# Two hybrid decoder layers: a gate tile asked for between the state-space halves, the first weights between the halves of x, decay and rate products of stacked exact parts, lag products in four runs

## The chip, the cores and the metric

The kernel runs on one core of a Trainium2 chip. The metric is the device time of one execution in microseconds (us); the time of a kernel is the median of its runs. Five engines work side by side, each through its own list of instructions in order: PE (TensorE, matrix products), DVE (VectorE), ACT (ScalarE), POOL (GpSimd) and SP (SyncE, which here starts the transfers).

## The reference

x (512 tokens by 1024 channels, float32) goes through two layers. Each layer projects x once and runs three token mixers on the projection; gates merge them, and a projection, two layer norms and an MLP follow. Shapes: A has 8 heads of 64; B 4 heads of 128 and 256; C 32 groups of 16 channels with 64 complex states each.

```python
proj = x @ w_in[l]
z_a, q_b, k_b, v_b, g_b, u_c, gate_logits = split(proj)
# A, rwkv7: zw, za, zg are 64, 64 and 128 columns of the token-shifted z_a
w_ll = -softplus(-(w0 + tanh(zw) @ w2)) - 0.5      # decay, w2 is 64 x 512
a = sigmoid(a0 + za @ a2)                          # rate,  a2 is 64 x 512
...                                                # delta rule over time
# B: retention.  C, state space: x[t] = ab * x[t-1] + bb @ u[t] (complex, diagonal)
y = gelu(real(c @ x) + d_skip * u)
y_c = y * sigmoid(y @ w_glu + b_glu)
merged = gate_a * (y_a @ wb_a) + gate_b * (y_b @ wb_b) + gate_c * (y_c @ wb_c)
x = layer_norm(alpha * x + merged @ w_out[l])
x = layer_norm(alpha * x + square(relu(x @ w_ff1[l])) @ w_ff2[l])
```

## The kernel before

**Large products.** Activations are held as a high part and a rest (xh, xl), both in a shortened float32 that TensorE multiplies exactly; weights too (wh, wl). A product is then three matmuls: wh by xh (L169), wh by xl (L170), wl by xh (L171). Weights come in blocks of 0.5 MB: `wblk` starts the transfer into raw (L148), ACT casts raw to wh (L151), DVE subtracts to wl (L155). raw, wh and wl each have three buffers in turn. A block of 128 channels gives 24 matmuls of 512 columns into one bank of the accumulator memory.

**Order.** A scheduler takes the recorded instructions, follows dependencies and priorities, and writes each engine's list; `ahead` raises the priority of what is recorded inside it, and `after` adds a dependency between two instructions. In the middle of a layer `weave` sets PE's order by hand: the chains of A and B are generators that yield (PE time, wait), and a filler of large matmuls (gates, B's projection, branch products) is put between their pieces.

**Start.** Four tiles of x (xin) are loaded, transposed on PE (`put_xT`, L219, four matmuls per accumulator bank, two banks per tile), cast and split. The three first weight blocks of u (the state space's columns) are loaded behind them on SP's list. For u each block is worked through in two halves of 256 tokens.

**State space (C).** `s5_prep` makes matrices from the parameters while PE runs u's and A's projections: transposes L402 (eight groups of four per layer) and, into one bank, the lag products L411 (32 matmuls of 32 rows by 128 per layer; a run of four is one value of (m, part)). `s5_main` works on two halves of the states: products with u (L460) into banks m and p, scans and twists on DVE that end in x (tiles cx, last instruction L484), then y of the half in two banks b: 64 matmuls of 64 columns on cx (L490) and 32 on u (L495); then gelu (L500 to L504) writes cy. Banks b are two, so y of half 1 can be written when gelu of half 0 has read both. The first three gate tiles (`gates`, L1088; each 24 large matmuls, then a tanh on ACT) are recorded behind `s5_main`, and the scheduler fills PE's waits with them. `s5_glu` follows.

**Decay and rate (A).** `a_proj` leaves the 128 rows of tanh(zw) and za in one float32 tile. `a_prep` of each of the four pairs of heads multiplies them with w2a2 (w2 and a2 stacked, loaded in `a_setup`, L633 and L634): one float32 matmul of the upper 64 rows (L671), one of the lower 64 (L675), 512 columns each, each into a bank m (of two). The bank is read by ACT. Ahead of them stand products of the pair before (L776, AVX, also into a bank m, read by ACT L777).

Of the kernel before, what the change touches and what calls it, by code (L numbers as in the profile page):

```python
# [11 lines left out]
F32 = mybir.dt.float32  # L12
# [68 lines left out]
class Hybrid:  # L81
# [61 lines left out]
    def wblk(self, src, a_, b_, extra=None):  # L143

        nc = self.nc
        with self.ahead(-2000000):
# [159 lines left out]
    def s5_prep(self, pool, keep):  # L306
# [64 lines left out]
        for d, b in zip(bd, (bre, bim)):  # L371
            G.memset(d, 0.0)
            for h in range(2):
                S.copy(out=d[H[h], :, h, :], in_=b[H[h]])

# [3 lines left out]
        for q in range(4):  # L379
# [16 lines left out]
            mix(self.ca[1][:, r], 9, 0, cim, cre, ADD, neg=True)  # L396
            for part, (x_, y_, op) in enumerate(((bre, bim, SUB), (bim, bre, ADD))):
                bp = t("bp", (128, 4, 8, 16))
                mix(bp, 8, 0, x_, y_, op)
                ps = self.mps()  # L400
                for i in range(4):
                    PE.transpose(ps[:, 128 * i:128 * i + 128], bp[:, i].rearrange("p b c -> p (b c)"), self.ident)  # L402
                S.copy(out=self.ba[:, part, r, :], in_=ps.rearrange("p (i s) -> p i s", i=4))

        gs = t("gs", (128, 4, 256))
        G.memset(gs[:, :, 0:128], 0.0)
        ps = self.pps().rearrange("p (m x) -> p m x", m=4)
        for m in range(4):
            for part in range(2):
                for j in range(4):  # L410
                    PE.matmul(ps[32 * j:32 * j + 32, m, :], lhsT=bd[part][:, 4 * m + j].rearrange("p g c -> p (g c)"),  # L411
                              rhs=self.ca[part][:, 4 * m + j, 0:8, :].rearrange("p k c -> p (k c)"), start=part == 0,
                              stop=part == 1, tile_position=(0, 32 * j))
        S.copy(out=gs[:, :, 128:256], in_=ps)
# [10 lines left out]
    def s5_u(self, pool):  # L425
# [9 lines left out]
        blocks = [self.wblk(w[:, :, C_U + 128 * i:C_U + 128 * i + 128], 8, 128) for i in range(3)]  # L435
# [9 lines left out]
    def s5_main(self, pool, keep):  # L445
# [7 lines left out]
        for hf in range(2):  # L453
# [31 lines left out]
            yp = [self.bps(), self.bps()]  # L485
# [6 lines left out]
            for g in range(2):  # L492
                for i in range(8):
                    gr = 2 * (8 * hf + i) + g
                    PE.matmul(yp[g][:, 64 * i:64 * i + 64], lhsT=self.tt[:, gr, :], rhs=self.uc[:, gr, :],  # L495
                              start=False, stop=True, skip_group_check=True)
            for g in range(2):

                ps, y, g1 = yp[g], page("cy", 2), page("cg1")
                S.activation(g1, ps, AF.Square)  # L500
                V.tensor_scalar(g1, g1, 0.044715, 1.0, op0=MUL, op1=ADD)
# [101 lines left out]
    def a_proj(self, pool, gp):  # L603
# [6 lines left out]
        def consume(i, ps):  # L610
            az, bg = dict(tag="az%d" % max(0, i - 11), bufs=1), dict(tag="bg", bufs=3)
            t, s = (p.tile([128, T], F32, name=self.nm(n), **k) for p, n, k in
                    ((gp, "az", bg) if i < 12 else (pool, "az", az), (pool, "azs", az) if i < 12 else (gp, "azs", bg)))
# [6 lines left out]
            elif i == 12:  # L620
                nc.scalar.activation(t[0:64], t[0:64], AF.Tanh)
                self.zwa = t
# [7 lines left out]
    def a_setup(self, pool):  # L630
        nc, par = self.nc, self.par
        self.w2a2 = pool.tile([128, T], F32, tag="w2a2", name=self.nm("w2a2"))
        nc.sync.dma_start(out=self.w2a2[0:64], in_=self.a["a_w2"][self.l])  # L633
        nc.sync.dma_start(out=self.w2a2[64:128], in_=self.a["a_a2"][self.l])  # L634
# [9 lines left out]
        for s in self.sbd:  # L644
            nc.gpsimd.memset(s, 0.0)

    def a_prep(self, pool, keep, p):
# [23 lines left out]
        PE.matmul(ps, lhsT=self.w2a2[0:64, 128 * p:128 * p + 128], rhs=self.zwa[0:64, :], start=True, stop=True)  # L671
# [3 lines left out]
        PE.matmul(ps, lhsT=self.w2a2[64:128, 128 * p:128 * p + 128], rhs=self.zwa[64:128, :], start=True, stop=True)  # L675
# [10 lines left out]
        yield 1.7, 1.0  # L686
# [93 lines left out]
    def a_inv(self, pool, p):  # L780
# [6 lines left out]
        NL = page("NL", 2, (128, 16, 16))  # L787
# [14 lines left out]
    def a_post(self, pool, p, bank):  # L802
# [71 lines left out]
        GM = page("GM", 2, (128, 8, 128))  # L874
# [283 lines left out]
    def layer(self, l):  # L1158
# [4 lines left out]
        if l == 0:  # L1163
            with tc.tile_pool(name="xin", bufs=1) as xin:
                self.new_xT()
                for t in range(4):
                    x = xin.tile([128, D], F32, tag="xin", bufs=4, name=self.nm("xin"))
                    with self.ahead(-3000000):
                        nc.sync.dma_start(out=x, in_=src[128 * t:128 * t + 128])
                    self.put_xT(t, x)  # L1170
# [178 lines left out]
```

## Time and profile before

| | us |
|---|---|
| median of 3 runs | 2098.81 |
| the runs | 2094.45, 2098.81, 2101.46 |
| the profiled execution, its own time | 2095.62 |
| its span in the profile | 2093.8 |

| engine | busy share of the span |
|---|---|
| PE | 98% |
| DVE | 58% |
| ACT | 35% |
| POOL | 7% |

A row of a timeline is: start, duration, engine, line, operation, tile written, tiles read, tile sizes, number of instructions in the group, and in brackets how long the engine was idle before it and what ended that. Matmuls overlap, so a group's duration is longer than the distance to the next one; distances between starts are used below. One operation of float32 can show as more than one matmul record. PEclk is TensorE's granted clock as a share of 2.4 GHz, 0.50 is 1.2 GHz.

### The profile page before, as it was taken

What the parts mean: (1) busy time and instruction counts of PE and PEld (TensorE: products, weight loads), DVE (VectorE), ACT (ScalarE), POOL (GpSimd) and SP (SyncE); (2) the same over time, 40 slices, a digit from 0 to 9 for tenths busy, and PEclk for the clock granted to TensorE, in tenths of its full rate; (3) what the DMA queues carried; (4) which work ended last, traced back from release to release, by engine and by line L of the source; (5) the groups of instructions that cost most, each with busy time, mean ns of one, the idle gap of its engine ahead of it and who ended that gap; (6) DMA issues with size and microseconds to landing.
All of it is one profiled execution on the core that took longest, in us unless ns stands there. A gap on an engine that the chain in (4) does not pass through costs nothing.

```text
span 2093.8 us, 31704 instructions
## 1 busy us (share of the span) xinstructions
PE 2061.0 (98%) x12784; PEld 1705.9 (81%) x12784; DVE 1217.3 (58%) x2048; ACT 741.4 (35%) x1079; POOL 147.8 (7%) x302
## 2 busy tenths in 40 slices
PE   8999999999999999999999999999999999999998
PEld 7788888788877888888887888888888878888886
DVE  7763567785566634344596644687856666343345
ACT  5433443434232423233244234344443324132231
POOL 0300022022000000000013000221120000000000
PEclk9998999999999999999999999999999999999999
DMA  9694643423645323233275856433336534223231
GB/s 221 155 140 142 183 127 82 112 78 88 223 150 177 113 79 121 81 100 110 93 159 158 127 151 183 123 94 88 100 113 191 178 130 140 79 93 101 91 121 50
DMA packets 365170, 263.95 MB, mean 126 GB/s; under 512 B 79328, under 2 KB 309856, under 8 KB 364896
## 3 DMA queue, kind: packets, MB, share of 16 engines
q1 hardware_dynamic: 365024, 261.93, 45.0%
q8 instruction: 100, 1.64, 0.3%
q14 instruction: 46, 0.38, 0.1%
HBM read 218.89 MB, written 42.99 MB: 125 GB/s over the span
## 4 chain that ended last, share of the span: by engine, by line
PE 86%; DVE 6%; DMA 3%; ACT 2%; issue 2%; SPq 1%; DVEq 0%; ACTq 0%
PE g L169 24%; PE g L170 24%; PE g L171 24%; PE b L1048 2%; DVE wl L155 1%; PE p L907 1%; PE m L736 1%; PE b L1028 1%; SPq L506 1%; PE b L171 1%; PE b L170 1%; PE p L880 1%; PE b L169 1%; PE p L910 1%; ACT wh L151 1%
## 5 line engine op out<-in xcount | busy, mean ns | idle before, releaser
L151 ACT CAST wh<-raw 128x1024 fp32r<-128x1024 f32 x312 | 326.4, 1051 | 788.6 <-PE g L170 354.3
L155 DVE TENSOR_TENSOR wl<-raw,wh 128x1024 fp32r<-128x1024 f32 x312 | 382.4, 1230 | 344.1 <-ACT wh L151 338.1
L169 PE MATMUL g<-xh,wh 128*128 128x512 f32 (+1 forms) x1472 | 574.0, 390 | 5.8 <-ACT wh L151 3.0
L170 PE MATMUL g<-xl,wh 128*128 128x512 f32 (+1 forms) x1472 | 562.9, 383 | 0.2
L171 PE MATMUL g<-xh,wl 128*128 128x512 f32 (+1 forms) x1472 | 562.1, 382 | 0.0
L169 PEld LDWEIGHTS g<-xh,wh 128*128 128x128 f32 x1472 | 277.1, 188 | 67.4 <-issue 7.3
L171 PEld LDWEIGHTS g<-xh,wl 128*128 128x128 f32 x1472 | 277.4, 189 | 54.5 <-issue 1.0
L170 PEld LDWEIGHTS g<-xl,wh 128*128 128x128 f32 x1472 | 277.8, 189 | 53.9 <-issue 3.5
L170 PE MATMUL g<-wl,hh 128*128 128x512 f32 x512 | 201.2, 394 | 1.1 <-DVE wl L155 1.1
L171 PE MATMUL g<-wh,hl 128*128 128x512 f32 x512 | 201.1, 393 | 0.0
L169 PE MATMUL g<-wh,hh 128*128 128x512 f32 x512 | 200.2, 392 | 0.0
L170 PEld LDWEIGHTS g<-wl,hh 128*128 128x128 f32 x512 | 96.3, 188 | 24.1 <-DVE wl L155 2.0
L169 PEld LDWEIGHTS g<-wh,hh 128*128 128x128 f32 x512 | 96.2, 188 | 22.0
L171 PEld LDWEIGHTS g<-wh,hl 128*128 128x128 f32 x512 | 96.2, 188 | 21.3
L169 PE MATMUL g<-yh,wh 128*128 128x512 f32 x256 | 102.6, 401 | 0.7 <-ACT yh L176 0.7
L1291 DVE TENSOR_TENSOR yb<-yb,g 128x512 f32<-128x512 f32 x48 | 32.9, 686 | 120.8 <-PE g L171 120.6
L170 PE MATMUL g<-yl,wh 128*128 128x512 f32 x256 | 100.6, 393 | 1.9 <-DVE yl L177 1.9
L171 PE MATMUL g<-yh,wl 128*128 128x512 f32 x256 | 100.7, 393 | 0.0
L796 POOL TENSOR_TENSOR TLt<-NL,TL 128x120 f32<-128x120 f32 (+14 forms) x120 | 50.8, 423 | 599.6 <-DMA NL<-nsc 590.8
L169 PE MATMUL g<-wh,xh 128*128 128x256 f32 x256 | 77.0, 301 | 0.7 <-DVE bsw L981 0.6
L170 PE MATMUL g<-wl,xh 128*128 128x256 f32 x256 | 72.3, 283 | 0.0
L171 PE MATMUL g<-wh,xl 128*128 128x256 f32 x256 | 72.3, 282 | 0.0
(346 smaller groups left out, 2731.2 us busy)
## 6 DMA issues: line engine op xcount, KB each, us to landing
raw<-in_w_in SPq DMA_DIRECT2D x132, 512.0 KB, 4.2
raw<-in_w_ff SPq DMA_DIRECT2D x128, 512.0 KB, 4.2
raw<-in_w_branch SPq DMA_DIRECT2D x32, 512.0 KB, 4.3
gs<-gth SPq DMA_DIRECT2D x48, 256.0 KB, 2.6
gth<-gs SPq DMA_DIRECT2D x48, 256.0 KB, 3.1
raw<-in_w_out SPq DMA_DIRECT2D x16, 512.0 KB, 4.9
zs<-az SPq DMA_DIRECT2D x24, 256.0 KB, 4.2
s5tt<-gsc SPq DMA_DIRECT2D x16, 256.0 KB, 11.9
```

The source lines that it names most:

```text
L151: nc.scalar.copy(out=wh, in_=raw)
L155: eng.tensor_tensor(wl, raw, wh.bitcast(F32), op=SUB)
L169: mm(out, lhsT=wh, rhs=xh, start=first, stop=False)
L170: mm(out, lhsT=wh, rhs=xl, start=False, stop=False)
L171: mm(out, lhsT=wl, rhs=xh, start=False, stop=last)
L506: nc.sync.dma_start(out=out[t, :, g, prs], in_=n8(y)[16 * t:16 * t + 16])
L736: PE.matmul(ps[h][:, i, :].rearrange("p (s i) -> p s i", i=64), lhsT=BK[H[h], c, :], rhs=rhs, start=True, stop=True)
L796: G.tensor_tensor(tmp[:, :, 0:n], NL[:, s:s + 1, s + 1:16].to_broadcast([128, 8, n]), TL[:, :, s:s + 1].to_broadcast([128, 8, n]), op=MUL)
L880: PE.matmul(ps[H[h], i, :].rearrange("p (s i) -> p s i", i=64), lhsT=Pt[H[h], 4 * g + i, :], rhs=AVX[H[h], h:3:2 - h, 4 * g + i, :], start ...
L907: PE.matmul(ps[:, h, :], lhsT=AB[:, h, c, :], rhs=AVX[:, h, c, :], start=h == 0, stop=c == 0, skip_group_check=True)
L1048: PE.matmul(po[ic // 2][:, ic % 2, :], lhsT=sT[jc][:, o:o + 128], rhs=v[:, jc, :], start=jc == 0, stop=jc == ic)
L1291: V.tensor_tensor(y[t][:, s], y[t][:, s], ps, op=ADD)
```

## The change

What it does, in the order of the diff: `wblk` gets a higher priority for two first blocks of u, and `layer` records them between the second and third tile of x. The lag products go in four runs, each behind the transposes of one quarter, held there by `after`. `s5_main` takes the generator of the gates and records one gate tile between x and y of half 1; y of half 1 goes to banks m and p instead of b. The float32 pair for decay and rate becomes, for each of the two, two matmuls of 128 rows: a tile holds high part and rest of the activation one above the other (azz), and the high part of the weight is stacked twice, its rest twice (lora), which gives all four products of parts. The weights take the slot of a raw block, in `a_lora`, called just ahead of `weave`. The planner's time for this step goes from 1.7 to 1.0. NL and GM have one buffer where they had two.

```diff
@@ wblk
-    def wblk(self, src, a_, b_, extra=None):
+    def wblk(self, src, a_, b_, extra=None, first=False):
 
         nc = self.nc
-        with self.ahead(-2000000):
+        with self.ahead(-3500000 if first else -2000000):
             raw = self.wp.tile([128, a_, b_], F32, tag="raw", bufs=3, name=self.nm("raw"))
...
@@ s5_prep
+        pg = self.pps().rearrange("p (m x) -> p m x", m=4)
+        def lags(m):
+            for part in range(2):
+                for j in range(4):
+                    PE.matmul(pg[32 * j:32 * j + 32, m, :], lhsT=bd[part][:, 4 * m + j].rearrange("p g c -> p (g c)"),
+                              rhs=self.ca[part][:, 4 * m + j, 0:8, :].rearrange("p k c -> p (k c)"), start=part == 0,
+                              stop=part == 1, tile_position=(0, 32 * j))
+                    ins = nc.cur_bb.bb.instructions[-1]
+                    if self.run is not None:
+                        self.after(ins, self.run)
+                    self.run = ins
...
+            self.run = None
+            if q == 3:
+                lags(3)
...
+                    if q < 3:
+                        self.run = nc.cur_bb.bb.instructions[-1]
...
+            if q < 3:
+                lags(q)
 
         gs = t("gs", (128, 4, 256))
         G.memset(gs[:, :, 0:128], 0.0)
-        ps = self.pps().rearrange("p (m x) -> p m x", m=4)
-        for m in range(4):
-            for part in range(2):
-                for j in range(4):
-                    PE.matmul(ps[32 * j:32 * j + 32, m, :], lhsT=bd[part][:, 4 * m + j].rearrange("p g c -> p (g c)"),
-                              rhs=self.ca[part][:, 4 * m + j, 0:8, :].rearrange("p k c -> p (k c)"), start=part == 0,
-                              stop=part == 1, tile_position=(0, 32 * j))
-        S.copy(out=gs[:, :, 128:256], in_=ps)
+        S.copy(out=gs[:, :, 128:256], in_=pg)
@@ project u
-        blocks = [self.wblk(w[:, :, C_U + 128 * i:C_U + 128 * i + 128], 8, 128) for i in range(3)]
+        early = self.early if self.l == 0 else []
+        blocks = early + [self.wblk(w[:, :, C_U + 128 * i:C_U + 128 * i + 128], 8, 128) for i in range(len(early), 3)]
@@ s5_main
-    def s5_main(self, pool, keep):
+    def s5_main(self, pool, keep, gates):
...
-            yp = [self.bps(), self.bps()]
+            yp = [self.bps(), self.bps()] if hf == 0 else [self.mps(), self.pps()]
+            insts, of = nc.cur_bb.bb.instructions, lambda e, n: [i for i in insts[n:] if i.engine == e]
+            at = len(insts)
+            if hf:
+                ahead = of(mybir.EngineType.PE, 0)[-1]
+                for _ in range(9):
+                    next(gates)
+                tile_ = of(mybir.EngineType.PE, at)
+                tanh = of(mybir.EngineType.Activation, at)[-1]
+                self.after(tile_[0], ahead)
+                at = len(insts)
...
+            if hf:
+                self.after(of(mybir.EngineType.PE, at)[0], tile_[-1])
...
+                if hf and g == 0:
+                    self.after(insts[-1], tanh)
@@ a_proj
-                    ((gp, "az", bg) if i < 12 else (pool, "az", az), (pool, "azs", az) if i < 12 else (gp, "azs", bg)))
+                    ((gp, "az", bg) if i < 13 else (pool, "az", az), (pool, "azs", az) if i < 12 else (gp, "azs", bg)))
...
-                self.zwa = t
+                H = (slice(0, 64), slice(64, 128))
+                self.zwa = [pool.tile([128, T], F32R, tag="az%d" % j, bufs=1, name=self.nm("azz")) for j in range(2)]
+                for h, o, z in zip(H, H[::-1], self.zwa):
+                    nc.scalar.copy(out=z[h], in_=t[h])
+                    nc.vector.tensor_tensor(z[o], t[h], z[h].bitcast(F32), op=SUB)
@@ a_setup, a_lora
-        self.w2a2 = pool.tile([128, T], F32, tag="w2a2", name=self.nm("w2a2"))
-        nc.sync.dma_start(out=self.w2a2[0:64], in_=self.a["a_w2"][self.l])
-        nc.sync.dma_start(out=self.w2a2[64:128], in_=self.a["a_a2"][self.l])
...
+    def a_lora(self, pool):
+        nc = self.nc
+        raw = self.wp.tile([128, 2, T], F32, tag="raw", bufs=3, name=self.nm("raw"))
+        self.lora = []
+        for i, n in enumerate(("a_w2", "a_a2")):
+            for h in (slice(0, 64), slice(64, 128)):
+                nc.sync.dma_start(out=raw[h, i, :], in_=self.a[n][self.l])
+            wh, wl = (pool.tile([128, T], F32R, tag="l%s%d" % (x, i), name=self.nm("lora")) for x in "hl")
+            nc.scalar.copy(out=wh, in_=raw[:, i, :])
+            nc.vector.tensor_tensor(wl, raw[:, i, :], wh.bitcast(F32), op=SUB)
+            self.lora.append((wh, wl, self.zwa[i]))
@@ a_prep
-        PE.matmul(ps, lhsT=self.w2a2[0:64, 128 * p:128 * p + 128], rhs=self.zwa[0:64, :], start=True, stop=True)
+        s = slice(128 * p, 128 * p + 128)
+        lora = lambda wh, wl, z: (PE.matmul(ps, lhsT=wh[:, s], rhs=z, start=True, stop=False),
+                                  PE.matmul(ps, lhsT=wl[:, s], rhs=z, start=False, stop=True))
+        lora(*self.lora[0])
         S.activation(ld, ps, AF.Tanh, scale=0.5, bias=self.hw0[:, p:p + 1])
         V.tensor_scalar(ld, ld, -0.5 * EH, -0.5 * EH, op0=MUL, op1=ADD)
         ps = self.mps()
-        PE.matmul(ps, lhsT=self.w2a2[64:128, 128 * p:128 * p + 128], rhs=self.zwa[64:128, :], start=True, stop=True)
+        lora(*self.lora[1])
         S.activation(a, ps, AF.Tanh, scale=0.5, bias=self.hw0[:, 4 + p:5 + p])
...
-        yield 1.7, 1.0
+        yield 1.0, 1.0
@@ a_inv, a_post
-        NL = page("NL", 2, (128, 16, 16))
+        NL = page("NL", 1, (128, 16, 16))
-        GM = page("GM", 2, (128, 8, 128))
+        GM = page("GM", 1, (128, 8, 128))
@@ layer
+                xs = []
                 for t in range(4):
-                    x = xin.tile([128, D], F32, tag="xin", bufs=4, name=self.nm("xin"))
-                    with self.ahead(-3000000):
-                        nc.sync.dma_start(out=x, in_=src[128 * t:128 * t + 128])
-                    self.put_xT(t, x)
+                    xs.append(xin.tile([128, D], F32, tag="xin", bufs=4, name=self.nm("xin")))
+                    with self.ahead(-3600000 if t < 2 else -3000000):
+                        nc.sync.dma_start(out=xs[t], in_=src[128 * t:128 * t + 128])
+                for t in range(2):
+                    self.put_xT(t, xs[t])
+                w = a["w_in"][l].rearrange("(k p) c -> p k c", p=128)
+                self.early = [self.wblk(w[:, :, C_U + 128 * i:C_U + 128 * i + 128], 8, 128, first=True) for i in range(2)]
+                for t in range(2, 4):
+                    self.put_xT(t, xs[t])
...
-                        self.s5_main(cm, cpl)
-                        for _ in self.gates(gp, 0, EARLY):
+                        early = self.gates(gp, 0, EARLY)
+                        self.s5_main(cm, cpl, early)
+                        for _ in early:
                             pass
...
-                self.share = 0
+                self.a_lora(ap)
```

SP's list at the start of the program, first before, then after (xin: a tile of x; raw: a weight block).

```order
L98 DMA ident<-in_kconst 128x128
L1169 DMA xin_86<-in_x 128x1024
L1169 DMA xin_102<-in_x 128x1024
L1169 DMA xin_118<-in_x 128x1024
L1169 DMA xin_134<-in_x 128x1024
L148 DMA raw_168<-in_w_in 128x8x128
L148 DMA raw_174<-in_w_in 128x8x128
L148 DMA raw_180<-in_w_in 128x8x128
```

The same place after:

```order
L98 DMA ident<-in_kconst 128x128
L1219 DMA xin_86<-in_x 128x1024
L1219 DMA xin_88<-in_x 128x1024
L148 DMA raw_122<-in_w_in 128x8x128
L148 DMA raw_128<-in_w_in 128x8x128
L1219 DMA xin_90<-in_x 128x1024
L1219 DMA xin_92<-in_x 128x1024
L148 DMA raw_180<-in_w_in 128x8x128
```

Two weight blocks have moved ahead of two tiles of x; the third has kept its place.

PE's list at y of the state space in layer 0, before: the end of y of half 0 (b_1292 and b_1293), the large matmuls of a gate tile (g_1606), the start of y of half 1 (b_1432).

```order
L490 MATMUL b_1293<-cx_216_1281,s5ca_73_514 128x64
L495 MATMUL b_1292<-uc_376,s5tt_678 128x64 x8
L495 MATMUL b_1293<-uc_376,s5tt_678 128x64 x8
L169 MATMUL g_1606<-xh_84,wh_1602 128x512
L170 MATMUL g_1606<-xl_85,wh_1602 128x512
L171 MATMUL g_1606<-xh_84,wl_1604 128x512
...
L171 MATMUL g_1606<-xh_84,wl_1604 128x512
L169 MATMUL g_1606<-xh_84,wh_1602 128x512
L490 MATMUL b_1432<-cx_233_1420,s5ca_72_513 128x64
L490 MATMUL b_1432<-cx_234_1421,s5ca_73_514 128x64
```

The same place after: the end of gate tile 1 (g_1480), the start and the end of y of half 0 (b_1295, b_1296), the start of y of half 1 (m_1435, p_1436).

```order
L171 MATMUL g_1480<-xh_84,wl_1478 128x512
L517 MATMUL b_1295<-cx_216_1283,s5ca_73_514 128x64
L517 MATMUL b_1296<-cx_216_1283,s5ca_73_514 128x64
L169 MATMUL g_1609<-xh_84,wh_1605 128x512
L517 MATMUL b_1295<-cx_217_1284,s5ca_74_515 128x64
...
L522 MATMUL b_1295<-uc_376,s5tt_678 128x64 x8
L522 MATMUL b_1296<-uc_376,s5tt_678 128x64 x8
L517 MATMUL m_1435<-cx_234_1423,s5ca_73_514 128x64
L517 MATMUL p_1436<-cx_234_1423,s5ca_73_514 128x64
```

Before, 19 of the 24 matmuls of the third gate tile stood between the two y (14 of them left out); after, one of them stands within y of half 0, and y of half 1 follows y of half 0 at once. The gate tile of the diff stands ahead of y of half 0. Layer 1 has the same order.

PE's list at the decay and rate products of the second pair in layer 0, before:

```order
L171 MATMUL g_2410<-xh_84,wl_2408 128x512
L776 MATMUL m_2467<-AVX_2431,AA_2303 64x64 x16
L671 MATMUL m_2539<-az_1184,w2a_111_688 128x512
L675 MATMUL m_2543<-az_1184,w2a_111_688 128x512
L169 MATMUL g_2410<-xh_84,wh_2406 128x512
```

The same place after:

```order
L171 MATMUL g_2428<-xh_84,wl_2426 128x512
L825 MATMUL m_2485<-AVX_2449,AA_2321 64x64 x16
L718 MATMUL m_2557<-azz_1187,lora_1908 128x512
L719 MATMUL m_2557<-azz_1187,lora_1909 128x512
L718 MATMUL m_2562<-azz_1188,lora_1914 128x512
L719 MATMUL m_2562<-azz_1188,lora_1915 128x512
L169 MATMUL g_2428<-xh_84,wh_2424 128x512
```

The place is the same; two matmuls have become four, into the same two banks m.

## Rows read from the trace of the kernel before

**Rows 1.** Page, part 1: busy time, share of the span, instructions.

```profile
PE 2061.0 (98%) x12784; PEld 1705.9 (81%) x12784; DVE 1217.3 (58%) x2048; ACT 741.4 (35%) x1079; POOL 147.8 (7%) x302
```

**Rows 2.** Timeline of PE and then ACT at the start of the program.

```profile
4.89 1.09 PE L219 MATMUL m<-ident,xin 128*128 128x128 f32 x4 [4.89 <-DMA xin<-in_x]
...
10.26 0.60 PE L219 MATMUL p<-ident,xin 128*128 128x128 f32 x4
...
14.34 0.38 PE L169 MATMUL g<-xh,wh 128*128 128x256 f32 x1 [1.25 <-ACT wh L151]
...
14.97 1.05 ACT L151 CAST wh<-raw 128x1024 fp32r<-128x1024 f32 x1 [0.69 <-DMA raw<-in_w_in]
```

**Rows 3.** Timeline of PE at the first run of lag products, layer 0.

```profile
65.26 0.39 PE L171 MATMUL g<-xh,wl 128*128 128x512 f32 x1
65.49 0.39 PE L169 MATMUL g<-xh,wh 128*128 128x512 f32 x1
65.81 0.43 PE L411 MATMUL p<-s5ca,s1bd 128*32 128x128 f32 x8
66.16 0.50 PE L170 MATMUL g<-xl,wh 128*128 128x512 f32 x1
```

**Rows 4.** Timeline of PE at y of both halves, layer 0, then layer 1.

```profile
137.06 3.79 PE L490 MATMUL b<-cx,s5ca 64*128 64x64 f32 x64
...
144.37 0.48 PE L169 MATMUL g<-xh,wh 128*128 128x512 f32 x1
...
152.99 7.06 PE L490 MATMUL b<-cx,s5ca 64*128 64x64 f32 x54 [2.03 <-DVE cy L504]
159.98 7.09 PE L495 MATMUL b<-uc,s5tt 128*128 128x64 f32 x32
...
1205.38 0.77 PE L170 MATMUL g<-xl,wh 128*128 128x512 f32 x1
```

**Rows 5.** Windows: stretch, length, PE busy (instructions), granted clock, DMA share, GB/s.

```profile
144.00:152.00 8.00, 6.26 (x35) 1.00 0.41 111
...
154.00:168.00 14.00, 14.00 (x86) 0.50 0.25 60
...
1194.00:1207.00 13.00, 13.00 (x77) 0.50 0.24 60
```

**Rows 6.** Timeline of DVE: the instruction that ends x of half 1, both layers.

```profile
146.32 0.68 DVE L484 TENSOR_TENSOR cx<-cx,c 128x504 f32<-128x504 f32 x1
...
1186.00 0.68 DVE L484 TENSOR_TENSOR cx<-cx,c 128x504 f32<-128x504 f32 x1
```

**Rows 7.** Timeline of PE at decay and rate of pairs 0 and 1, layer 0.

```profile
227.16 0.69 PE L671 MATMUL m<-az,w2a 64*128 64x512 f32 x1
227.17 0.69 PE L675 MATMUL m<-az,w2a 64*128 64x512 f32 x1
...
228.22 0.50 PE L169 MATMUL g<-xh,wh 128*128 128x512 f32 x1
...
281.84 1.12 PE L671 MATMUL m<-az,w2a 64*128 64x512 f32 x2
282.59 1.12 PE L675 MATMUL m<-az,w2a 64*128 64x512 f32 x2
283.65 0.50 PE L169 MATMUL g<-xh,wh 128*128 128x512 f32 x1
```

**Rows 8.** Waits of PE: tile and line, what ended them, us, times, longest.

```profile
PE b L490 <- DVE cy L504: 4.9, 4, 2.0
...
PE g L170 <- DVE yl L177: 1.9, 2, 1.0
```

**Rows 9.** Page, part 5 (busy, mean ns, idle before) and part 6 (KB, us to land).

```profile
L151 ACT CAST wh<-raw 128x1024 fp32r<-128x1024 f32 x312 | 326.4, 1051 | 788.6 <-PE g L170 354.3
L155 DVE TENSOR_TENSOR wl<-raw,wh 128x1024 fp32r<-128x1024 f32 x312 | 382.4, 1230 | 344.1 <-ACT wh L151 338.1
...
raw<-in_w_in SPq DMA_DIRECT2D x132, 512.0 KB, 4.2
```

## Prediction

> **What bounds the kernel now.** First the page's busy shares: PE is busy for 98% of the span, no other engine for more than 58% [rows 1]. So time comes back only where PE waits, or where it works at a bad price. Next I read PE's waits: its idle time is 2093.8 − 2061.0 = 33 us, and the longest entries are the banks of y, 4.9 us in four [rows 8], the start, and the operands of branch B's first tile, 1.9 us. Then the timelines of the places that the diff touches [rows 2 to 4, 7], to see what one step costs PE beyond its matmuls; and the windows for the granted clock [rows 5], because two stretches run at 1.2 GHz, and they are just those in which y of half 1 stands. A large matmul starts 0.23 us after the one before it (65.26 to 65.49) [rows 3]; this step prices whatever moves.
>
> The sum is made against the profiled execution's own 2095.62 us, 3.2 under the median; the same difference is put to the median.
>
> **Start-up.** Seven equal transfers of 0.5 MB land between 4.89 and 14.97, so one each (14.97 − 4.89) / 6 = 1.68 us. Steady large matmuls begin at 14.34, when the second weight block is cast [rows 2]. In the new order the first block is third in the row: it lands at 4.89 + 2 × 1.68 = 8.25, its cast takes 1.05 [rows 2] and the rest of the split 1.23 [rows 9], so the large matmuls begin with all three kinds at about 10.6, 3.7 us earlier. The sixteen transposes of the third and fourth tile, in four groups of four, have not gone away; they stand now between the large matmuls. A group costs about 0.44 at the full clock (the last of before shows 0.60 with its overlap) and 0.85 at the low one (1.09 with overlap) [rows 2]: 1.8 to 3.4. That gives 3.7 − 1.8 = 1.9, or 3.7 − 3.4 = 0.3 where the clock comes late, since PE now pauses between 8 and 10. I take −1.6, nearer the warm price, as the last groups of before are warm already; range −3 to +0.5. It reaches the end because PE is full from here to the first y.
>
> **Lag products.** A run of four costs 66.16 − 65.49 − 0.23 = 0.44 us, of which 0.32 − 0.23 = 0.09 is the seam ahead of it, and I add as much for the seam behind [rows 3]: 0.53. Layer 0 has eight such runs: 4.2 us. After, the 32 matmuls stand behind transposes, which have their seams already: eight fours of 66.16 − 65.81 = 0.35 and two seams make 3.0. Against that, two more places per layer cut the products with u apart, each two seams: +0.3. So 0.9 a layer, −1.8 in all; range −2.6 to −0.8 (a bound in which each run keeps both its seams).
>
> **Decay and rate.** Pair 0: the two float32 products of 64 rows each start 0.01 us apart and both are gone after 228.22 − 227.16 = 1.06 us [rows 7]. They run side by side in the two halves of the array. Pairs 1 to 3 (pair 1 stands for them): the second starts 282.59 − 281.84 = 0.75 after the first and the next large matmul 1.06 after that, 1.81 in all [rows 7]; there the second waits for the bank of the AVX products, which ACT has still to read. A layer costs 1.06 + 3 × 1.81 = 6.5. After: four large matmuls, 4 × 0.23 = 0.92 for pair 0; for the others the second two still wait out the 0.75, then 2 × 0.23: 1.21. That is 0.92 + 3 × 1.21 = 4.55, 1.95 less a layer, 3.9 in two. The new matmuls are of the kind of their neighbours, so the seams of 0.09 at eight places go too: −0.8. I take −4.7. Ends: only pair 0 gains, (1.06 − 0.92) + 0.2 a layer, −0.7 in all; or the bank wait falls away too, 4 × 0.92 = 3.7 against 6.5 and seams, −6.4. The Trainium skill, "TensorE: Matmul & The Clock Gate", part 3, on packing small matmuls by rows, says that products in different row groups run at the same time, which speaks against replacing such a pair. Rows 7 bear it out for pair 0; by the rule alone all four pairs would cost 1.06 before and the change would give about −1; the 1.81 of pair 1 shows that the bank takes the overlap away there. The new casts and subtractions, four and four a layer, lie on ACT and DVE, which are idle for 65% and 42% of the span [rows 1]; they cost nothing unless their slot in the weight ring is missed (below).
>
> **State-space halves.** In the order after, no gate tile stands between the two y: 19 large matmuls that did stand there come behind. So the banks no longer hold y of half 1 back, its x does: that is ready at 146.32 + 0.68 = 147.0, and 0.4 earlier since a weight block ahead on DVE lands earlier: 146.6. In layer 1 it is 1186.0 + 0.68 = 1186.7 [rows 6]. y of half 0 ends at 144.37 [rows 4], so PE stands idle for 2.2 us there. Before, after a wait of 2.03 at the same place, the clock went from full to 0.50 for the whole of y of half 1, in both layers [rows 4, 5]. I expect the same again. At the low clock y of half 1 takes 166.8 − 153.0 = 13.8 for 54 + 32 records, and some 1.3 for the ten that ran ahead: 15.1. Layer 0: 146.6 + 15.1 = 161.7, then the 18 matmuls still due, 18 × 0.23 = 4.1: 165.8, against 166.8 before (159.98 + 7.09, less the overlap of 0.25): −1.0. Layer 1: 1186.7 + 15.1 + 4.1 = 1205.9 against 1205.4 [rows 4]: +0.5. Together −0.5; range −4 to +3.5, from one us of idle more or less per layer and from the clock coming back earlier or later behind it. The 4.9 us of bank waits [rows 8] thus do not come back: the wait for x takes their place, and the clock takes the rest.
>
> **The rest.** Branch B's first tile costs 1.9 in two waits [rows 8]; after, some 21 large matmuls of the filler come behind the last piece of the chains instead of ahead, 21 × 0.23 = 4.8 us of cover. I take half, −1.0; range −2.5 to 0. One buffer of NL and GM instead of two: each pair's use ends before the next pair's begins; if not, the wait lies on POOL and DVE beside a filled PE. I cost it at nothing.
>
> **Sum.** −1.6 − 1.8 − 4.7 − 0.5 − 1.0 = −9.6: the profiled execution comes to 2086.0, the median to 2089.
>
> **Rivals.** (a) *The clock holds.* If the pause of 2.2 us does not lower it, y of half 1 takes as long as that of half 0, 144.37 − 137.06 = 7.3 instead of 15.1, and the large matmuls behind it are at the full clock at once, about 1 us more: 8.8 a layer. In both layers 2089 − 17.6 = 2071; in one 2080. For it: in after there is one pause, where layer 0 had two close together. Against it: the 2.03 in both layers of before, with the same small matmuls behind [rows 4, 5]. The Trainium skill, same page, table under "Why this matters for your kernels", asks that no long idle gaps be left between bursts of matmuls, and the gaps it means are longer than these; by it the clock would hold and the time would be 2071. This trace disagrees: 2.03 us came ahead of a fall from 1.00 to 0.50. 8% for both layers, 6% for one.
>
> (b) *The ring of weights runs dry: slower.* The lora tile takes one of three raw slots from its load, well ahead of the weave, until it is split. If weight blocks run on two slots or one meanwhile, a block costs 4.2 (landing) + 1.05 + 1.23 = 6.5 [rows 9] where PE takes 24 × 0.23 = 5.5. With one slot left, some 8 blocks a layer would lose 1.0 each, +16 in two layers, and the time is 2105. It decides from the point where the tile's split is late by more than one block. For it: the tile's loads stand on the same queue and its split waits for az. Against it: casts wait for PE 354 of their 789 idle us [rows 9], so the ring has slack, and a second slot stays free. 6%.
>
> (c) *The change does not give what it says.* Decay and rate gain only what pair 0 shows (−0.7), the transposes at the start run cold (−0.3), branch B gives nothing, y as above (−0.5), lag products −1.5: −3.0, that is 2096. For it: the bank wait remains in six of eight places, of which [rows 7] show one. 20%.
>
> **How the numbers follow.** My forecast has the remaining 60%, with its own range 2083 to 2093. Each of the ends sums about one us of every term. A measurement of this kernel tells about 0.3%, 6.3 us, from no change, so faster means under 2092.5. The forecast gives 57 of its 60 to faster, (a) all 14, (c) 2 of 20; (b) is the slower case. So faster 0.73, same 0.21, slower 0.06. The range 2077 to 2096 leaves out (a) in both layers, (b), and a little at the edges of (c).
>
> **What would show it.** In the trace after: large matmuls in a row from about 10.6 with transposes among them; four runs of lag products a layer, each right behind a group of transposes; four matmuls of 0.23 at decay and rate, with a wait of about 0.3 between the second and the third in pairs 1 to 3; y of half 1 starting close to 146.6 − 4 (all before it moves by start-up and lag products) behind an idle of about 2.2; the windows there at 0.50 in both layers. It is wrong if the clock stays at 1.00 there (then by 8.8 a layer), if the casts wait for DMA at the start of the weave, or if the chains' first pieces, shifted by the planner's new 1.0, arrive late and PE waits where it did not.

## The result and the profile after

The changed kernel takes 2111.4 us (median of 4 runs, 2108.7 to 2113.0) against 2096.6 for the kernel before: 1.0069 times, 95% interval 1.0057 to 1.0081, 14.8 us slower. The forecast was 2089. In the profiled executions the span goes from 2093.8 to 2106.9.

PE's busy time has hardly moved ([rows 1]); its idle time went from 33 to 46 us. Page, part 1, of the changed kernel:

```profile
PE 2060.6 (98%) x12784; PEld 1713.2 (81%) x12784; DVE 1221.8 (58%) x2056; ACT 747.6 (35%) x1087; POOL 152.4 (7%) x302
```

To find the place, I laid the two timelines side by side by the large matmuls (L169 to L171), of which both kernels have 8160 records, with the same tiles at all but 103 places of the sequence: the difference in the start of the 100th, the 500th and so on says how much each stage won or lost. Worked out in this way, in us, after minus before:

| stage, by the number of large matmuls | changed kernel |
|---|---|
| layer 0: start, to the 100th | −0.1 |
| projections of u and A, lag products, to the 500th | −0.5 |
| state space and first gates, to the 700th | +5.6 |
| woven part and branches, to the 2700th | +2.5 |
| the rest of layer 0 and layer 1's start, to the 4200th | +0.3 |
| layer 1: projections, lag products, to the 4600th | −0.8 |
| state space and first gates, to the 4900th | +1.2 |
| woven part and branches, to the 6200th | +5.1 |
| the rest | −0.4 |

The loss has two seats, the two state-space stages (+6.9 together) and the two woven parts (+7.6); the decay and rate products lie in the second. PE's waits in the changed kernel (the columns as in [rows 8]):

```profile
PE g L169 <- ACT gth L1137: 7.9, 2, 6.3
...
PE p L883 <- DVE T L870: 4.6, 2, 2.3
PE m L751 <- ACT ao L748: 2.6, 4, 1.2
PE m L795 <- DVE AA L789: 2.1, 4, 0.6
PE p L959 <- DVE sbd L964: 1.9, 4, 0.7
PE m L517 <- DVE cx L498: 1.8, 2, 1.3
PE m L517 <- DVE cx L499: 1.7, 2, 0.9
```

The waits for cy of [rows 8] are gone, and so are those for yl. In their place stand 3.5 us for x of half 1 (cx), a wait that the forecast had (2.2 us in layer 0; 1.43 came), and two kinds that the forecast did not have: 7.9 us for a gate's tanh (gth), and some 11 us for pieces of A's chains (T, ao, AA, sbd) in the woven part.

**Woven part.** The longest new wait in layer 0, PE and then DVE, and the windows behind it:

```profile
460.17 0.74 PE L883 MATMUL p<-T,AD 32*32 32x32 f32 x64 [2.30 <-DVE T L870]
```

```profile
459.58 0.45 DVE L870 STREAM_TRANSPOSE T<-PD 128x256 f32<-128x256 f32 x1
```

```profile
460.90:463.00 2.10, 2.10 (x7) 0.64 0.03 8
463.00:465.00 2.00, 2.00 (x6) 0.53 0.00 0
```

**State space.** Timeline of PE, layer 0, then windows (stretch, length, PE busy, granted clock, DMA share, GB/s):

```profile
144.92 0.29 PE L517 MATMUL m<-cx,s5ca 64*128 64x64 f32 x1 [0.56 <-DVE cx L498]
...
146.23 0.29 PE L517 MATMUL m<-cx,s5ca 64*128 64x64 f32 x1 [0.87 <-DVE cx L499]
...
155.22 3.62 PE L522 MATMUL p<-uc,s5tt 128*128 128x64 f32 x16
158.60 0.77 PE L170 MATMUL g<-xl,wh 128*128 128x512 f32 x1
...
182.66 0.80 PE L169 MATMUL g<-xh,wh 128*128 128x512 f32 x1 [6.27 <-ACT gth L1137]
```

```profile
150.00:155.00 5.00, 5.00 (x33) 0.50 0.33 53
155.00:160.00 5.00, 5.00 (x21) 0.50 0.29 48
...
165.00:170.00 5.00, 5.00 (x24) 1.00 0.23 38
...
182.00:186.00 4.00, 3.34 (x8) 0.50 0.55 153
```

y of half 1 starts behind a pause of 0.56 + 0.87 us, runs at 0.50 of the clock and ends at 158.6: the forecast's mechanism. Then PE does 23 + 24 + 24 large matmuls, at 1.00 again in the third window, and stops at 176.4 for 6.27 us; with this pause the clock falls a second time, as the last window shows. What it waited for stands in ACT's timeline, after:

```profile
169.90 0.69 ACT L1137 ACTIVATE gth<-g,hbg 128x512 f32<-128x512 f32 x1
178.36 0.63 ACT L179 ACTIVATE cyhl<-cyg 128x512 fp32r<-128x512 f32 x1 [7.78 <-DMA cyg<-yst]
180.45 0.63 ACT L179 ACTIVATE cyhl<-cyg 128x512 fp32r<-128x512 f32 x1 [1.46 <-DMA cyg<-yst]
...
181.92 0.68 ACT L1137 ACTIVATE gth<-g,hbg 128x512 f32<-128x512 f32 x1
```

and before:

```profile
170.40 0.67 ACT L1088 ACTIVATE gth<-g,hbg 128x512 f32<-128x512 f32 x1
...
175.88 0.68 ACT L1088 ACTIVATE gth<-g,hbg 128x512 f32<-128x512 f32 x1
180.55 0.63 ACT L179 ACTIVATE cyhl<-cyg 128x512 fp32r<-128x512 f32 x1 [3.99 <-DMA cyg<-yst]
```

Before, the tanh of the fourth gate tile stood ahead of the two splits of y (cyhl), which wait for a transfer. After, it stands behind them, though its tile was done at 170.6. A gate tile needs one of two banks; the bank that this tanh had to free was missed. (Eight gate tiles are recorded around `s5_main` in both kernels, EARLY in the kernel's head, not three as the part on the kernel before says; so there are a fourth and a seventh.)

### The profile page after: what moved, and what is told of

Read it like the earlier page. It is cut to its first block, busy times and chain, and to the rows that moved or that the text cites. A ratio compares the mean times of both kernels' runs of the same rounds, so it can differ in the third digit from the quotient of the medians.

```text
span 2106.9 us, 31716 instructions
## 1 busy us (share of the span) xinstructions
PE 2060.6 (98%) x12784; PEld 1713.2 (81%) x12784; DVE 1221.8 (58%) x2056; ACT 747.6 (35%) x1087; POOL 152.4 (7%) x302
## 4 chain that ended last, share of the span: by engine, by line
PE 82%; DVE 9%; DMA 4%; ACT 2%; issue 2%; SPq 1%; DVEq 0%; ACTq 0%
PE g L169 24%; PE g L170 23%; PE g L171 23%; DVE wl L155 2%; DMA raw<-in_w_in 1%; PE p L956 1%; PE b L1097 1%; ACT wh L151 1%; PE b L1077 1%; PE b L171 1%; PE b L170 1%; PE p L929 1%; PE b L169 1%; SPq L537 1%; PE p L959 1%
## 5 line engine op out<-in xcount | busy, mean ns | idle before, releaser
L169 PE MATMUL g<-xh,wh 128*128 128x512 f32 (+1 forms) x1472 | 578.4, 393 | 12.0 <-ACT gth L1137 7.9
L171 PE MATMUL g<-xh,wl 128*128 128x512 f32 (+1 forms) x1472 | 564.6, 384 | 0.5 <-DVE wl L155 0.5
L169 PEld LDWEIGHTS g<-xh,wh 128*128 128x128 f32 x1472 | 279.4, 190 | 71.4 <-ACT gth L1137 9.1
L171 PEld LDWEIGHTS g<-xh,wl 128*128 128x128 f32 x1472 | 279.4, 190 | 55.3 <-DVE wl L155 0.8
L171 PE MATMUL g<-wh,hl 128*128 128x512 f32 x512 | 201.1, 393 | 0.0
L169 PE MATMUL g<-wh,hh 128*128 128x512 f32 x512 | 200.2, 392 | 0.0
L170 PEld LDWEIGHTS g<-wl,hh 128*128 128x128 f32 x512 | 96.3, 188 | 24.4 <-DVE wl L155 2.3
L169 PEld LDWEIGHTS g<-wh,hh 128*128 128x128 f32 x512 | 96.2, 188 | 22.0
L171 PEld LDWEIGHTS g<-wh,hl 128*128 128x128 f32 x512 | 96.1, 188 | 21.2
L169 PE MATMUL g<-yh,wh 128*128 128x512 f32 x256 | 102.2, 399 | 0.0
L171 PE MATMUL g<-yh,wl 128*128 128x512 f32 x256 | 99.9, 390 | 0.0
L169 PE MATMUL g<-wh,xh 128*128 128x256 f32 x256 | 75.6, 295 | 0.8 <-DVE bsw L1030 0.8
L171 PE MATMUL g<-wh,xl 128*128 128x256 f32 x256 | 72.3, 282 | 0.0
```

Source lines behind the costliest of these rows:

```text
L169: mm(out, lhsT=wh, rhs=xh, start=first, stop=False)
L170: mm(out, lhsT=wh, rhs=xl, start=False, stop=False)
L171: mm(out, lhsT=wl, rhs=xh, start=False, stop=last)
```

## The experiments

Each is given with its difference from the kernel that it starts from. The kernel before was timed beside each group; its median was 2096.7, 2096.8, 2096.7 and 2098.3.

**e1, from the changed kernel: the splits of half 1 behind the fourth gate tile's tanh.**

```diff
-        for m in range(4):
-            y = page("cyg", 4)
...
+        late((0, 1))
+        self.late = late
...
                         for _ in early:
                             pass
+                        self.late((2, 3), self.tanhs[3])
```

`late`, whose own lines are not shown, makes the same loads and splits and holds ACT's part of a split behind the instruction that it is given, here the tanh of the fourth gate tile. The splits of half 0 stay where they were.

> The changed kernel with one thing moved: ACT's two splits of y of half 1 (cyhl from cyg) stand behind the tanh of the fourth gate tile, not ahead of it; PE's list keeps its order. Theory A (a late gate tanh behind a split that waits for a transfer): PE's wait of 6.27 us at 182.66 in layer 0 and the 1.67 us at 1227.87 in layer 1 go, and with the first the low clock behind it (some 2 to 3 us more); about 9 to 11 us less than the changed kernel, near 2101. Rival B (the low clock in y of half 1 is what costs): y of half 1 is as slow as ever, and the time stays within 2 us of the changed kernel's 2111.

Measured: 2100.5 us, 1.0019 of before (1.0008 to 1.0030), 10.9 less than the changed kernel. PE's timeline shows the long wait gone, and the second tanh is ahead of the splits again (ACT):

```profile
184.09 0.50 PE L169 MATMUL g<-xh,wh 128*128 128x512 f32 x1 [1.01 <-ACT gth L1144]
```

```profile
172.97 0.68 ACT L1144 ACTIVATE gth<-g,hbg 128x512 f32<-128x512 f32 x1
178.61 0.63 ACT L179 ACTIVATE cyhl<-cyg 128x512 fp32r<-128x512 f32 x1 [4.96 <-DMA cyg<-yst]
```

PE's list is the same, instruction by instruction, and y of half 1 still runs at 0.50. So theory A holds. Of the 10.9 the profiles place 7.6 in the two state-space stages (+5.6 and +1.2 become +0.5 and −1.2) and 1.6 in a start that happened to be faster, so the order on ACT costs 8 to 11 of the 14.8.

**e2, from the changed kernel: the planner's number back.**

```diff
-        yield 1.0, 1.0
+        yield 1.7, 1.0
```

> The changed kernel with the planner's time for the decay and rate step put back from 1.0 to 1.7, so that PE's order in the woven part is that of the kernel before. Theory C (the planner's other number made an order in which the chains are late): PE's new waits in the woven part, T 2.30, ao 0.96, sbd 0.35, bg 0.49 and AA 1.05 us in layer 0 and the like in layer 1, fall back to about 0.5 a layer, the waits for yh and yl of branch B (1.6 us and a stretch of low clock) come back, and the time is 5 to 8 us less, about 2105. Rival D (one buffer of NL and GM instead of two holds the inverse and its followers back): the waits for T and sbd stay with the old order too, and the time is within 2 us of 2111.

Measured: 2111.0, no change. By the total theory C had failed; by stages it had not. The woven part of layer 0 goes from +2.5 to −2.3 and that of layer 1 from +5.1 to +0.7. What ate the gain is layer 1's state space, +12.3 for +1.2: y of half 0 met a pause of 2.00 us there and ran at the low clock as well, after a wait of 2.5 us for azs. This wait for azs comes again in e5 below. So the total of this run mixes two things, and e6 was made to separate them.

**e6, from the kernel before: the planner's number alone.** The same instructions, 1.0 in place of 1.7.

> The kernel before with one number changed: the planner's time for the decay and rate step 1.0 in place of 1.7; the same instructions. Theory C: the order that it makes is the late one; in the traces the changed kernel lost 2.5 and 4.7 us in the two woven parts in spite of 2.0 gained by the products in each, so the order alone costs 4.5 and 6.7: about 2107. Rival D (the single buffers, which this kernel does not have): no change, 2097.

Measured: 2110.2, 1.0061 (1.0048 to 1.0074), 13.3 us slower. PE's waits:

```profile
PE p L834 <- DVE T L821: 5.0, 2, 2.7
...
PE p L910 <- DVE sbd L915: 2.6, 4, 1.1
...
PE m L746 <- DVE AA L740: 2.1, 4, 0.7
```

These are the woven part's waits of the changed kernel, with two buffers of NL and GM and without any new product. Theory C holds and rival D falls: 5.7 and 5.3 us, 11.0 of the 13.3, lie in the two woven parts. In the changed kernel the longest of these waits ends at 460.17: DVE reaches the transposition T only at 459.58, behind other chains' work that fills it from 451.5 with one gap of 0.41 us. In the two windows behind it the granted clock is 0.64 and 0.53, so there a wait of 2.3 us costs more than its length.

**e4, from the changed kernel: s5_main as before** (y of half 1 in banks b, gates behind).

> The changed kernel with s5_main as before: y of half 1 in banks b, no gate tile held, the gates all behind it; the rest of the change as it is. The two traces put the loss of the state-space part at 5.6 us in layer 0 and about 0.9 in layer 1, so theory A expects 4 to 8 us less than the changed kernel, about 2105, with waits for cy of about 2 us and the low clock as before. If the loss sits elsewhere (rivals B and D) the time stays at 2111.

Measured: 2104.9, 1.0035 (1.0021 to 1.0048), 6.5 less than the changed kernel. Layer 0's state space loses nothing any more (−0.4 for +5.6), the rest of the loss stays in the woven parts.

**e3, from the changed kernel: large matmuls really between the halves.**

```diff
-                ahead = of(mybir.EngineType.PE, 0)[-1]
+                for _ in range(18):
+                    next(gates)
+                at = len(insts)
                 for _ in range(9):
-                    next(gates)
+                    next(gates, None)
...
-                self.after(tile_[0], ahead)
+                self.after(tile_[0], self.y0)
...
+            self.y0 = of(mybir.EngineType.PE, at)[-1]
```

A step of `gates` is three large matmuls. The first eighteen stay free; the next nine are held behind the last matmul of y of half 0 (`self.y0`).

> The changed kernel with the third gate tile and three eighths of the fourth held behind y of half 0 and ahead of y of half 1 (32 large matmuls, 7.3 us), the first two tiles free. Theory E (the pause of 1.4 to 2.2 us ahead of y of half 1 lowers the clock): no pause, y of half 1 at the full clock in about 7.4 us instead of 14, in both layers; with the wait behind the gate tanh gone too the time is 15 to 25 us under the changed kernel, 2086 to 2096. Rival F (two runs of small matmuls lower the clock whether or not PE pauses): the windows at y of half 1 show 0.50 again and the gain is at most the 10 us of the late tanh.

Measured: 2094.9, 0.9993 (0.9984 to 1.0003), 16.5 less than the changed kernel. Windows at y of half 1 in layer 0, and its last matmuls:

```profile
144.00:150.00 6.00, 6.00 (x28) 1.00 0.07 13
150.00:154.00 4.00, 4.00 (x54) 1.00 0.41 71
154.00:158.00 4.00, 4.00 (x47) 1.00 0.30 49
```

```profile
155.00 2.00 PE L524 MATMUL m<-uc,s5tt 128*128 128x64 f32 x16
156.84 1.95 PE L524 MATMUL p<-uc,s5tt 128*128 128x64 f32 x16
```

No pause, clock 1.00, y of half 1 in 7.3 us where the changed kernel took 12.4 from its second wait on. Theory E holds: the kernel before also has large matmuls between the halves, 19 for the 32 here, but a pause of 2.03 us ahead of y of half 1, and there the clock is 0.50 [rows 4, 5]. Rival F falls as far as runs of small matmuls with large ones between go; two such runs at once and without a pause stand in no kernel here. Two waits for a late tanh remain (3.93 and 4.65 us, and the clock falls with each).

**e7 and e8, from the kernel before: one part of the change each.** e7 has the stacked products with their slot and the single buffers, planner at 1.7; e8 the new start.

> The kernel before with the stacked decay and rate products, the weights' slot in the ring, and one buffer of NL and GM, the planner at 1.7. From the products' cost in the traces (13.2 us in eight places before, 9.2 after) the time is 4.0 us less, about 2092.7. Rival D: the single buffers eat it, 2096 or more. Rival (b) of the prediction (the ring of weights runs dry): 2105.

> The kernel before with the new start alone. In five traces of kernels with this start the hundredth large matmul stands between 2.0 us earlier and 0.6 us later than in the kernel before; the working of the prediction gave 0.3 to 1.9 earlier. Expected 2095 to 2097, a difference under one us; 2093 or less if the large matmuls between the transposes keep the clock up.

Measured: e7 2094.7, 0.9985 (0.9974 to 0.9995), 2 us by the medians and 3 by the ratio where the products alone give about 4; a few waits of under 1 us come back. e8 2095.5, 0.9993 (0.9985 to 1.0002): nothing that can be told. With the single buffers and the slot in the ring of weights e7 still gains 1 us at the weak end of its interval, so the two together cost at most some 3 us of the 4, and nothing that can be told.

**e5, from e3: 1.7, and the splits of y behind the tanhs of the fourth and the seventh tile.**

> The kernel of e3 (a real gate tile between the halves) with the planner's 1.7 of e2 and ACT's splits of y held behind later tanhs: those of half 0 behind the tanh of the fourth gate tile, those of half 1 behind that of the seventh. Theory A, C and E together: the waits of 3.93 and 4.65 us behind a late gate tanh go in both layers with the low clock behind them (7.0 and 5.4 us by the traces of e3), the woven part is as in e2 layer 0, 4 to 6 us a layer better than in e3; 2095 - 12 - 10 = about 2073, at most 2080. If the low clock at y is not tied to the pause, or the order of the woven part is not what costs there, it stays over 2085.

Measured: 2083.3, 0.9929 (0.9913 to 0.9944), ten more than expected. Layer 0 gives 11.9 in the state space; layer 1 loses 5.1 there. PE, then ACT:

```profile
1162.70 0.79 PE L169 MATMUL g<-xh,wh 128*128 128x512 f32 x1 [5.45 <-ACT azs L654]
```

```profile
1161.96 0.69 ACT L654 ACTIVATE azs<-g,par 128x511 f32<-128x511 f32 x1 [12.72 <-DMA zs<-az]
```

This is a third cost, which the edit of `a_proj` makes possible: with az of the decay and rate block moved into the ring bg, four tiles in a row want its three buffers, and the last of them waits for a store that lies among other transfers. In the changed kernel ACT waited 0.74 us there and PE not at all, so it is no part of the 14.8; e2 had paid it already.

**e9, from e5: azs of that block in slot az1.**

```diff
-                    ((gp, "az", bg) if i < 13 else (pool, "az", az), (pool, "azs", az) if i < 12 else (gp, "azs", bg)))
+                    ((gp, "az", bg) if i < 13 else (pool, "az", az), (pool, "azs", az) if i < 13 else (gp, "azs", bg)))
```

> e5 with one tile moved: azs of the decay and rate block in the slot az1 instead of the ring bg, as the changed kernel's move of az into that ring made the next azs wait for a store of az, which in layer 1 of e5 landed late (5.45 us of PE, and the low clock of 12 us behind it). PE's order is that of e5. Expected: no wait for azs, layer 1's y of half 0 at the full clock, 6 to 10 us less than e5: 2073 to 2077. Rival: the wait moves to another tile of the ring bg and the time stays at 2083.

Measured: 2067.5, 0.9850 (0.9831 to 0.9870): 1.5% under the kernel before, and faster than both. The two state-space stages stand at −11.9 and −11.1. Page, part 1, and the first waits of PE:

```profile
PE 2041.9 (99%) x12784; PEld 1695.4 (82%) x12784; DVE 1223.3 (59%) x2056; ACT 745.6 (36%) x1087; POOL 150.8 (7%) x302
```

```profile
PE m L219 <- DMA xin<-in_x: 5.4, 1, 5.4
PE g L170 <- DVE yl L177: 1.9, 2, 1.0
```

PE's list is that of e5. Against the kernel before, PE's busy time falls by 19 us. An estimate: leaving out the last microseconds of the program, the trace before has 34 us at 0.50 and this one 7, and half of the 27 is 13.6; the shorter products give the other 5 to 6.

**e10 to e12, from e9: the planner's number at 1.0, 1.2 and 2.2.**

> e9 with the planner's time for the decay and rate step at 1.0, as in the changed kernel. Theory C: the order loses as in e6, in both layers, about 10 to 13 us over e9, near 2086.

> e9 with the planner's time at 1.2, which is what the step costs by the traces (1.25 in pairs 1 and 2). If 1.0 is bad because it is below the price, this is as good as e9 (within 2 us). If the planner's clock has to run ahead of the sum of its prices, or the order is a matter of luck, it loses 3 us or more against e9.

> e9 with the planner's time for the decay and rate step at 2.2, half a microsecond over the 1.7 of e9 and near twice its price in the traces. So far 1.0 gave 2079.9, 1.2 gave 2075.7 and 1.7 gave 2067.5. If the planner's clock needs slack over the real price, 2.2 is as good as 1.7 or better, 2064 to 2068. If each number just gives another order, and 1.7 is the one that the other numbers were chosen with, it is worse, 2072 or more.

Measured: 2079.9, 2075.7 and 2073.8, for 2067.5 at 1.7. 1.0 costs 12.4, as in e6. 1.2 loses 8.2 and 2.2 loses 6.4, both with other waits (RT, Pt), so 1.7 is the best of the four by the total. The two woven parts, after minus before in one profile each, say something else about 2.2:

| planner's number | woven parts, layers 0 and 1 | both |
|---|---|---|
| 1.0 (e10) | +3.2, +5.7 | +8.9 |
| 1.2 (e11) | +1.2, +2.5 | +3.8 |
| 1.7 (e9) | −1.1, +2.0 | +0.9 |
| 2.2 (e12) | +0.2, +0.4 | +0.5 |

In the six profiles at 1.0 (after, e1, e3, e4, e6, e10) these parts stand at +6.9 to +12.8 us together, in the five at 1.7 (e2, e5, e7, e8, e9) at −4.1 to +0.9. That 1.0 is a bad number there is shown. Where the 6.4 us of 2.2 lie is not: its woven parts lose nothing against 1.7, and the profiled execution of e9 took 2072.1 us, 4.6 over its median. That 1.0 was simply below the price is not excluded either, since 1.2 is still a little under the 1.25 to 1.3 us that the step takes. Why 1.7 meets the other engines well stays open.

## Why the prediction was wrong, point by point

- **Start-up**, −1.6: wrong in size. The stage gave −0.1, and e8 nothing that can be told. The step that failed is the choice between 1.9 and 0.3 of gain: I took the warm price of a transposition group; the first group stood among large matmuls that were slow themselves. Timeline of PE, after:

```profile
12.74 0.41 PE L169 MATMUL g<-xh,wh 128*128 128x256 f32 x1
...
13.38 0.41 PE L169 MATMUL g<-xh,wh 128*128 128x256 f32 x1
13.59 0.96 PE L219 MATMUL m<-ident,xin 128*128 128x128 f32 x4
...
15.30 0.28 PE L169 MATMUL g<-xh,wh 128*128 128x256 f32 x1
...
15.66 0.28 PE L169 MATMUL g<-xh,wh 128*128 128x256 f32 x1
```

  Three matmuls take 0.64 us up to 13.4 and 0.36 from 15.3 on. They did begin at 9.8 instead of 14.3 ([rows 2]), but the early ones ran at little over half the pace. In e1 and e10, which have the same start, the step is 0.12 us from 11.4 on, the first group of transposes costs 0.44 and 0.43, and the stage gives −1.7 and −1.5, as the sum had it; in the nine other profiles with this start it gives −0.4 to +0.7. So the warm price came in two profiled executions of eleven.
- **Lag products**, −1.8: near. The stages gave −0.5 and −0.8, and 0.0 in e6, e7 and e8, which have the old lag products.
- **Decay and rate**, −4.7: near. Measured from the large matmul ahead to the second one behind, the step is 0.3 us shorter at pair 0 and 0.6 at each of the others (pair 3 read in e7, where its neighbours are those of before): −4.1 in the eight places. The seams at eight places are 8 × 0.09 = 0.7, not 0.8. Pair 1 after:

```profile
286.62 0.51 PE L718 MATMUL m<-azz,lora 128*128 128x512 f32 x1
286.97 0.39 PE L719 MATMUL m<-azz,lora 128*128 128x512 f32 x1
287.38 0.50 PE L718 MATMUL m<-azz,lora 128*128 128x512 f32 x1
287.72 0.39 PE L719 MATMUL m<-azz,lora 128*128 128x512 f32 x1
287.95 0.40 PE L169 MATMUL g<-xh,wh 128*128 128x512 f32 x1
```

  The wait for the bank is there, 287.38 − 286.62 = 0.76, as worked out.
- **State-space halves**, −0.5: the mechanism was right (x becomes the bound, the pause lowers the clock, y of half 1 is slow), the term wrong by some 7 us. The step that failed is "then the 18 matmuls still due": I followed PE and DVE and did not look at ACT's list behind the place. Two splits had moved ahead of one tanh there, and e1 shows what it costs: 8 to 11 us. Without it, in e1, the two stages come to −0.7, and the term had −0.5.
- **The rest**, −1.0: the waits for yl went, as said. (In layer 0 of the kernel before, the granted clock from 579.5 to 583.0, right behind such a wait, is 0.51: a third slow stretch beside the two that the prediction names.) But the planner's 1.7 to 1.0 had no term at all; this is the second step that failed. It stands only in the last sentence, as something that could make the forecast wrong. e6 prices it at 13.3 us, 11.0 of them in the woven parts: the largest single cost of the change. Neither this nor ACT's order accounts alone for the 24.4 us between the forecast −9.6 and the measured +14.8; 13.3 and 10.9 do so together, by addition. No run mends just these two, so this sum is not shown, and that it is so close is partly luck.
- **Rivals.** (a), the clock holds in spite of the pause: in no run. It holds in e3 and e9, where no pause is left; in e9 the two state-space stages stand at −11.9 and −11.1, for the 8.8 a layer that was worked out. (b), the ring of weights: no such wait is in the trace. (c): lag products and decay and rate gave most of what they promise; other things took it. The slower case that came had not been among them.

## What to carry to other kernels

When a change lets one engine finish earlier, read the lists of all the engines that serve it, over the next stage too: an instruction that waits for a transfer, set one place ahead of another that frees a buffer, can cost its whole wait. A number in a planner that orders thousands of instructions is an edit as large as any; try it alone, with the same instructions, and judge it by stages, because a total can hide a gain behind an unrelated loss. Fill a pause ahead of small matmuls with large ones rather than shorten it.

## What the runs showed of the hardware

- Pauses of 0.56 and 0.87 us, 1.3 us apart, ahead of and among the small matmuls of y were followed by the granted clock falling from 1.00 to 0.50. So it went in both layers of all eight kernels that pause ahead of y or in it there (before, after, e1, e2, e4, e6, e7, e8; 1.4 to 3.3 us of pause). The Trainium skill, "TensorE: Matmul & The Clock Gate", table under "Why this matters for your kernels", warns of longer pauses only; the traces here disagree.
- Among large matmuls a pause of that size lowers the clock in some places and not in others. The wait for T of 2.3 to 2.7 us stands twelve times in the six kernels at 1.0: with eight of them the clock falls to 0.50, with four it does not (both in e1, layer 0 of e4, layer 1 of e6). No run shows what decides.
- Two runs of 96 small matmuls of the state space with 32 or 33 large matmuls between and no pause kept 1.00 throughout (e3, e9, both layers): the pause, not the size, goes with the fall.
- At the start of the changed kernel large matmuls of 256 columns ran at 0.21 us a step up to 13.4 us and at 0.12 from 15.3 us, while the windows name a granted clock of 1.00 for both stretches. The trace holds no record of the clock ahead of 14.3 us, and the windows count a stretch without a record as 1.00. There the step between starts tells more.
